# DeltaNet flow step: the gate rows move in five GpSimd transfers instead of sixteen SyncE transfers

## The chip, the core and the metric

The kernel runs on one core of a Trainium2 chip, as one program in which five engines work side by side, each through a list of its own: TensorE (PE, with its weight loads as PEld), VectorE (DVE), ScalarE (ACT), GpSimd (POOL) and SyncE (SP). SP does nothing but issue transfers. ACT and POOL issue transfers too, between their other instructions. SP's and ACT's transfers run on hardware queues, POOL's on a software queue. Every engine works strictly in the order of its list: an instruction that waits holds up everything behind it on that engine. The metric is the device time of one execution in microseconds (us).

## What is computed

One layer of a flow-matching backbone, for 128 context tokens and 512 latent tokens. A conditioning vector gives shift, scale and gate for each half of the layer; the gate multiplies the normalised output before it is added back:

```python
sh1, sc1, g1, sh2, sc2, g2 = _adaln(c, w_ada[l], b_ada[l])   # silu(c) @ w_ada + b_ada, six rows of 1024
h = _rms(xs, norm_pre1[l]) * (1 + sc1) + sh1
y = _mixer_latent(h, ...)          # neighbourhood attention + bidirectional gated DeltaNet
xs = xs + g1 * _rms(y, norm_post1[l])
xs = _ffn_sub(xs, sh2, sc2, g2, norm_pre2[l], norm_post2[l], w_ff1[l], w_ff2[l])   # uses g2 * norm_post2
```

There are two conditioning vectors (context and latent), so the kernel needs four rows of 1024 numbers: g1 and g2, each for both vectors, each multiplied by the weight of the norm behind it (norm_post1, norm_post2).

## The kernel before

All 640 tokens stay on the chip as `hhi`/`hlo` (a rounded part and the rest, so that each product is three matmuls, lines 1002 to 1004). After the first projections come three stages that matter here. The **DeltaNet stage** runs ten chunk steps (`step`, lines 787 to 874); between the small matmuls of a step, slots are filled with matmuls of a dense stream (`Unit.run`, line 994), which makes the projections of the attention and of the sigmoid gates. The **attention stage** follows, with the rest of the dense stream in its slots, and then the output projection and the MLP. In the DeltaNet stage the order on PE, DVE, ACT and SP is that in which the code is written (a manual schedule); GpSimd's order, and that of instructions that the code writes further down but that may start early, is set by a scheduler.

A unit of the dense stream loads its weights with SP into a buffer `raw` (line 172), ACT rounds them to `whi` (line 941), DVE takes the difference to `wlo` (line 945), and the buffer is free again. In the last two chunk steps two `raw` buffers are in use, so the next load waits for the difference of the unit before. A finished product lies in one of two PSUM banks `ps_mm`; ACT copies it to `gth` (line 958, three buffers), SP stores it (`gt_d`, line 972). A bank can be written again when ACT has copied it.

The **gate rows**: eight extra units give g1 and g2 as columns; DVE adds the bias and writes them into `gcol` (line 1036). `gate_rows` (line 1045), which runs in the first free bank after the last of them, loads the matching bias-free factors norm_post into a `gth` buffer called `gbn`, 32 rows of 128 numbers (line 1049), transposes `gcol` on PE into the spare columns of the bank (line 1050), multiplies the two on DVE (line 1057), and stores the 32 rows to the DRAM tensor `g_d` (line 1054). `gate_bcast` reads `g_d` back much later, in the projection and at the end. The loads and stores are cut in eight because the columns of `gcol` are kept in the order (gate and quarter, half, vector), and `g_d` in the order (gate, vector, channel).

Around it in the DeltaNet stage: line 784 loads the right-hand side of a step, line 820 loads the other direction's output of the step (`ot`, or `kt` in the last step) from `o_d`, which DVE adds at line 841 and 864; line 883 (ACT) squares the sum, line 881 loads `z_d` for the norm behind it, line 924 stores the finished output to `od_d`. The attention's first loads are issued early: `vw` (line 1246, on POOL, sixteen before the attention starts), `qk` (line 1250), `cvt` and `vctx` (line 1303) and `bias` (line 1278). `rotate` (lines 1258 to 1272) turns `qk` on DVE. Line 612 is PE's transpose of a finished output, line 1322 the first matmul of the attention's scores.

A transfer also waits for a semaphore lane: SP's and ACT's transfers share eight lanes in turn, POOL's have eight of their own. A transfer is not issued before the one eight places ahead of it in its set has landed.

Of the kernel before, what the change touches and what calls it, by code (L numbers as in the profile page):

```python
# [9 lines left out]
F32 = mybir.dt.float32  # L10
# [4 lines left out]
ALU = mybir.AluOpType  # L15
# [3 lines left out]
P = 128  # L19
# [78 lines left out]
def body(ctx: ExitStack, tc: tile.TileContext, I, O, dbg=None):  # L98
    nc = tc.nc
    dbg = dbg or {}  # L100
    V, S, G, PE = nc.vector, nc.scalar, nc.gpsimd, nc.tensor
# [31 lines left out]
    def C(n):  # L133
        i, o, w = _CW[n]
        return cst[i][:, o : o + w]

    ident = C("ident")
# [37 lines left out]
    def split(raw, kt, n, pool=None, eng=V):  # L175

        pool = pool or wpool
        hi = pool.tile([P, 1024], F32R, tag="whi", name="whi")
        lo = pool.tile([P, 1024], F32R, tag="wlo", name="wlo")
        S.copy(hi, raw)  # L180
        eng.tensor_tensor(lo, raw, hi.bitcast(F32), op=ALU.subtract)  # L181
        return [x.rearrange("p (k n) -> p k n", k=kt) for x in (hi, lo)]
# [27 lines left out]
    g_d = tc.dram_tile([2, 2, D], F32, name="g_d")  # L210
# [33 lines left out]
    def ada_mod(pc, kk, dst, bcol, nsel, pool):  # L244
        V.tensor_scalar(dst[:, 0, kk], pc[:, 0:2], b_ada[:, bcol + kk : bcol + kk + 1], None, op0=ALU.add)
        t = pool.tile([P, 2], F32, tag="adat", name="adat", bufs=2)
        V.tensor_scalar(t, pc[:, 2:4], b_ada[:, bcol + 8 + kk : bcol + 9 + kk], 1.0, op0=ALU.add, op1=ALU.add)
        V.tensor_scalar(dst[:, 1, kk], t, npre[:, nsel * 8 + kk : nsel * 8 + kk + 1], None, op0=ALU.mult)
# [53 lines left out]
    with tc.tile_pool(name="xp", bufs=1, side="right") as xp:  # L302
# [7 lines left out]
        with tc.manual_schedule(engines={mybir.EngineType.SP}):  # L310
# [29 lines left out]
            for kk in range(KT + AHEAD):  # L340
# [17 lines left out]
                for t in range(5):  # L358
                    a, w = TILES[t]
# [37 lines left out]
    for half in range(2):  # L397
        a, w = HALVES[half]
# [9 lines left out]
    for t in range(5):  # L408
        a, w = TILES[t]
# [90 lines left out]
    for x in range(3):  # L500
        sT = (kqS[:, 1], kqS[:, 0], vT)[x]
        pss = ps_tb() if x == 0 else None
        for hp in range(HP):
# [5 lines left out]
            b = cvb[mt % 2]  # L509
# [69 lines left out]
    dn = dctx.enter_context(tc.tile_pool(name="dn", bufs=1, reuse_waits="tile"))  # L579
# [200 lines left out]
    def rhs(si, m):  # L780

        r = dn.tile([P, 512], F32, tag="r", name="r", bufs=2)
        for d, (sl, mm) in enumerate(halves(si, m)):
            nc.sync.dma_start(r[sl], vs_d[d, mm, sl])
        return r
# [144 lines left out]
    class Unit:  # L930
# [63 lines left out]
        def run(self):  # L994
            if self.ch == "d":
                yield from self.branch()
            for g in () if self.ch in "dn" else range(5 if self.ch == "v" else 2):
# [13 lines left out]
                for (ch, i, c), raws in zip(self.extra, self.raws):  # L1011
                    if g == 0:
                        self.rows = dn.tile([P, 256], F32, tag="arow", name="arow", bufs=1)
                    hs = slice(128 * g, 128 * g + 128)
                    for k in range(KT):
                        q = slice(32 * (k % 4), 32 * (k % 4) + 32)
                        PE.matmul(bank[q, 320:448], csl[:, k, :], raws[k // 4][:, k % 4, hs], start=(k < 4), stop=(k >= 4),  # L1017
                                  tile_position=(0, 32 * (k % 4)))
                    reads.append(lambda: S.copy(self.rows[:, hs], bank[:, 320:448]))  # L1019
                    if g == 1:  # L1020
                        finals.append(lambda bank, ch=ch, i=i: self.columns(bank[:, 448:452], ch, i))
                        if (ch, i) == ("a", 7):
                            finals.append(gate_rows)
# [5 lines left out]
        def columns(self, pc, ch, i):  # L1029

            for j in range(2):
                PE.matmul(pc[:, 2 * j : 2 * j + 2], self.rows[:, j * 128 : j * 128 + 128], C("sel"), start=True, stop=True)
            if ch == "m":
                return lambda: ada_mod(pc, i, mod2, 24, 1, gp)
            b = b_ada[:, 16 + 24 * (i // 4) + 2 * (i % 4) :][:, 0:2].unsqueeze(2).to_broadcast([P, 2, 2])
            return lambda: V.tensor_tensor(gcol[:, i], pc.rearrange("p (i r) -> p i r", i=2), b, op=ALU.add)

        def load_extra(self):
            self.raws = [[load_raw(I["w_ada"][c, :, b * 1024 : b * 1024 + 1024], tag=t).rearrange("p (k n) -> p k n", k=4)
                          for b, t in enumerate(("whi", "wlo"))] for _, _, c in self.extra]  # L1040

    gcol = dn.tile([P, 8, 2, 2], F32, tag="gcol", name="gcol")
    finals = []

    def gate_rows(bank):

        gn = gp.tile([P, 128], F32, tag="gth", name="gbn", bufs=3)[0:32]
        for i in range(8):
            nc.sync.dma_start(gn[4 * i : 4 * i + 4], I["gate_c"][i // 4, i % 4, 1].rearrange("r (i p) -> i r p", i=2))
        PE.transpose(bank[0:32, 320:448], gcol.rearrange("p a i r -> p (a i r)"), ident)  # L1050

        def store():
            for i in range(8):
                nc.sync.dma_start(g_d[i // 4, :, i % 4 * 256 : i % 4 * 256 + 256].rearrange("r (i p) -> i r p", i=2), gn[4 * i : 4 * i + 4])

        def read():
            V.tensor_tensor(gn, gn, bank[0:32, 320:448], op=ALU.mult)
            later(0, "end", store)

        return read  # L1060
# [26 lines left out]
    def later(slots, phase, f):  # L1087
        plan.setdefault((now[0] + slots, phase), []).append(f)
# [41 lines left out]
    with tc.manual_schedule(engines={E_.PE, E_.DVE, E_.Activation, E_.SP}):  # L1130
# [35 lines left out]
        r = rhs(0, PAIRS[0])  # L1166
        for n in range(5):
# [11 lines left out]
            r = rhs(2 * n + 1, PAIRS[n])  # L1179
# [6 lines left out]
            if n < 4:  # L1186
                slot(P1, elim=3)
                r = rhs(2 * n + 2, PAIRS[n + 1])
# [47 lines left out]
    with (  # L1236
# [161 lines left out]
        with tc.manual_schedule(engines={E_.PE, E_.DVE, E_.Activation, E_.SP}):  # L1398
            late[0] = 1
            rot, oraw, subs = rotations(1, xq), [], []  # L1400
            for j in range(-2, n + 1):
                hp, b = BLK[min(j + 2, n - 1)]
# [27 lines left out]
                if j in (1, 3):  # L1430
                    for x in oraw:
                        i = len(turned_o)
# [47 lines left out]
    for c in range(4):  # L1480
# [3 lines left out]
        for mi in range(2):  # L1484
            j = 2 * c + mi
            g = gs[KT + j]
            for t0, t1 in TG:
                sl = slice(t0 * 128, t1 * 128)
                w = (t1 - t0) * 128
# [260 lines left out]
    def w2_raw(g, kh, nh):  # L1750
        return load_raw(w2(g, kh, nh))
# [159 lines left out]
    with tc.tile_pool(name="fin", bufs=2, side="right", reuse_waits="tile") as fin_:  # L1911
        gB2 = gate_bcast(1, fin_)
        w = {(kh, nh): split(w2_raw(7, kh, nh), 2, 512) for nh in range(2) for kh in range(2)}
        for blk in (None, (0, 0), (1, 0), (0, 1), (1, 1)):
            r = 0 if blk is None else 1
# [130 lines left out]
```

## Time and profile before

| | us |
|---|---|
| median of three runs | 1113.4 |
| the three runs | 1113.16, 1113.4, 1120.03 |
| profiled execution | 1112.54 |
| its span, first to last instruction | 1109.9 |
| TensorE busy in the span | 1052.8 |
| VectorE / ScalarE / GpSimd busy | 847.0 / 520.0 / 316.8 |
| mean granted TensorE clock | 0.992 of full |

The busy times are sums over the whole span; the places where PE stands still are found in the chain of waits and in the timelines. All stretches below are given in us from the start of the profiled span. "Clock" is the granted TensorE clock as a share of 2.4 GHz.

### The profile page before, as it was taken

How to read it: one execution, taken by the hardware profiler on the slowest of the kernel's cores; microseconds unless marked ns; L12 is line 12 of the kernel's file. 1: busy time of each engine (PE TensorE's matmuls, PEld its weight loads, DVE VectorE, ACT ScalarE, POOL GpSimd, SP SyncE). 2: the span in 40 equal slices, each digit the busy share in tenths (PEclk: the TensorE clock that was granted, in tenths of full speed). 3: DMA queues.
4: the chain of work that ended last, by engine and by line, in shares of the span. 5: the costliest groups of instructions: out<-in, count | busy, mean ns of one | idle time of the engine just before them, and what ended most of it. 6: DMA issues, size and time to landing. Idle time of an engine off the chain costs nothing.

```text
span 1109.9 us, 25388 instructions
## 1 busy us (share of the span) xinstructions
PE 1052.8 (95%) x10289; PEld 941.1 (85%) x10289; DVE 847.0 (76%) x1649; ACT 520.0 (47%) x1148; POOL 316.8 (29%) x275
## 2 busy tenths in 40 slices
PE   4999999989998999979999999999999999999996
PEld 3779899978987898878888999998888889797975
DVE  6567898497786686467867576899798888979785
ACT  5435443435452643327774443665444444544532
POOL 1352312000000001102514325335344353525213
PEclk9999999999999999999999999999999999999999
DMA  9832013565654655647537542465556556545605
GB/s 323 309 122 63 26 39 121 180 217 180 199 188 149 220 168 158 164 141 221 162 117 241 194 174 93 117 171 152 148 154 169 160 150 162 158 136 152 190 20 152
DMA packets 72628, 176.43 MB, mean 159 GB/s; under 512 B 18920, under 2 KB 28424, under 8 KB 72512
## 3 DMA queue, kind: packets, MB, share of 16 engines
q1 hardware_dynamic: 56320, 135.44, 36.4%
q0 software_dynamic: 9648, 24.77, 11.0%
q10 hardware_dynamic: 6544, 14.61, 4.1%
q8 instruction: 81, 1.33, 0.5%
q14 instruction: 35, 0.29, 0.1%
HBM read 150.62 MB, written 24.12 MB: 157 GB/s over the span
## 4 chain that ended last, share of the span: by engine, by line
PE 67%; DVE 21%; ACT 4%; issue 3%; DMA 3%; SPq 1%; ACTq 0%; POOL 0%; DVEq 0%; POOLq 0%
PE ps_mm L1002 5%; PE ps_mm L1004 4%; PE ps_mm L1003 4%; DVE wlo L181 4%; PE ps_mm L1646 3%; DVE y L516 3%; PE ps_mm L1644 2%; PE ps_mm L1645 2%; PE ps_mm L200 2%; DVE R L1757 2%; PE ps_mm L201 2%; PE ps_mm L202 2%; PE ps_st L1646 2%; PE ps_st L1644 2%; PE ps_st L1645 2%
## 5 line engine op out<-in xcount | busy, mean ns | idle before, releaser
L1002 PE MATMUL ps_mm<-hhi,whi 128*128 128x320 f32 x384 | 130.7, 340 | 4.9 <-ACT gth L958 4.5
L1004 PE MATMUL ps_mm<-hhi,wlo 128*128 128x320 f32 x384 | 121.3, 316 | 0.0
L1003 PE MATMUL ps_mm<-hlo,whi 128*128 128x320 f32 x384 | 121.2, 316 | 0.0
L180 ACT CAST whi<-raw 128x1024 fp32r<-128x1024 f32 x82 | 85.1, 1046 | 32.3 <-PE ps_mm L1645 8.5
L181 DVE TENSOR_TENSOR wlo<-raw,whi 128x1024 fp32r<-128x1024 f32 x59 | 81.1, 1381 | 22.0 <-ACT whi L180 21.7
L1002 PEld LDWEIGHTS ps_mm<-hhi,whi 128*128 128x128 f32 x384 | 74.6, 194 | 12.4 <-ACT gth L958 4.7
L181 POOL TENSOR_TENSOR wlo<-raw,whi 128x1024 fp32r<-128x1024 f32 x23 | 56.4, 2454 | 80.2 <-ACT whi L180 80.1
L1003 PEld LDWEIGHTS ps_mm<-hlo,whi 128*128 128x128 f32 x384 | 74.6, 194 | 0.2
L1004 PEld LDWEIGHTS ps_mm<-hhi,wlo 128*128 128x128 f32 x384 | 74.6, 194 | 0.0
L200 PE MATMUL ps_mm<-hhi,whi 128*128 128x320 f32 x192 | 60.5, 315 | 0.7 <-ACT cvb L512 0.6
L201 PE MATMUL ps_mm<-hlo,whi 128*128 128x320 f32 x192 | 59.7, 311 | 0.0
L202 PE MATMUL ps_mm<-hhi,wlo 128*128 128x320 f32 x192 | 59.4, 309 | 0.0
L181 DVE TENSOR_TENSOR wlo<-S,whi 128x1024 fp32r<-128x1024 f32 x28 | 54.9, 1979 | 4.3 <-ACT whi L180 4.2
L1246 POOL DMA_DIRECT2D vw<-v_d x32 | 21.1, 676 | 128.8 <-ACT arow L1019 94.6
L181 DVE TENSOR_TENSOR wlo<-T,whi 128x1024 fp32r<-128x1024 f32 x28 | 43.9, 1567 | 15.2 <-ACT whi L180 15.2
L654 POOL DMA_DIRECT2D rls<-ai_d x10 | 5.4, 540 | 174.5 <-PE ps_tb L617 160.2
L945 DVE TENSOR_TENSOR wlo<-raw,whi 128x1024 fp32r<-128x1024 f32 x35 | 42.7, 1221 | 10.9 <-ACT whi L941 10.4
L516 DVE SCALAR_TENSOR_TENSOR y<-cvb,cw,y 128x644 f32<-128x644 f32 x48 | 45.4, 945 | 0.9
L180 ACT CAST whi<-T 128x1024 fp32r<-128x1024 f32 x28 | 29.4, 1049 | 33.9 <-PE ps_mm L1645 16.2
L180 ACT CAST whi<-S 128x1024 fp32r<-128x1024 f32 x28 | 28.8, 1051 | 23.9 <-PE ps_tb L202 12.3
L941 ACT CAST whi<-raw 128x1024 fp32r<-128x1024 f32 x35 | 36.5, 1047 | 7.1 <-issue 6.1
L958 ACT ACTIVATE gth<-ps_mm 128x320 f32<-128x320 f32 x32 | 13.9, 436 | 55.4 <-PE ps_mm L1017 38.2
(577 smaller groups left out, 3533.5 us busy)
## 6 DMA issues: line engine op xcount, KB each, us to landing
raw<-in_w_ff_dram SPq DMA_DIRECT2D x57, 512.0 KB
raw<-in_w_ada_dram SPq DMA_DIRECT2D x48, 512.0 KB
raw<-in_w_gate_dram SPq DMA_DIRECT2D x16, 512.0 KB
S<-in_w_ff_dram SPq DMA_DIRECT2D x14, 512.0 KB
T<-in_w_ff_dram SPq DMA_DIRECT2D x14, 512.0 KB
S<-in_w_ff_dram POOLq DMA_DIRECT2D x14, 512.0 KB, 5.6
T<-in_w_ff_dram POOLq DMA_DIRECT2D x14, 512.0 KB, 7.2
raw<-in_w_dn_dram SPq DMA_DIRECT2D x12, 512.0 KB
```

Source lines behind the costliest of these rows:

```text
L180: S.copy(hi, raw)
L181: eng.tensor_tensor(lo, raw, hi.bitcast(F32), op=ALU.subtract)
L200: PE.matmul(out, ah, bh, start=(i == 0), stop=False)
L201: PE.matmul(out, ah, bl, start=False, stop=False)
L202: PE.matmul(out, al, bh, start=False, stop=(i == n - 1))
L516: V.scalar_tensor_tensor(y, b[:, j : j + 644], cw[:, mt * 5 + j : mt * 5 + j + 1], y, op0=ALU.mult, op1=ALU.add)
L1002: PE.matmul(ps, ah, bh, start=(k == 0), stop=False)
L1003: PE.matmul(ps, ah, bl, start=False, stop=False)
L1004: PE.matmul(ps, al, bh, start=False, stop=(k == KT - 1))
L1644: PE.matmul(o, hi[:, k, fs], bh, start=(first and k == 0), stop=False, skip_group_check=not first)
L1645: PE.matmul(o, hi[:, k, fs], bl, start=False, stop=False, skip_group_check=not first)
L1646: PE.matmul(o, lo[:, k, fs], bh, start=False, stop=(k == 3), skip_group_check=not first)
```

## The change

The columns of `gcol` are kept in the order in which the rows of `g_d` follow each other: gate, vector, quarter, half. With that, the 32 rows of `gbn` are one contiguous block of `g_d`, so that one transfer stores them all, and four transfers of eight rows load the factors. All five are issued by GpSimd in place of SyncE.

```diff
-            return lambda: V.tensor_tensor(gcol[:, i], pc.rearrange("p (i r) -> p i r", i=2), b, op=ALU.add)
+            return lambda: V.tensor_tensor(gcol[:, i // 4, :, i % 4].rearrange("p r i -> p i r"), pc.rearrange("p (i r) -> p i r", i=2), b, op=ALU.add)
...
-    gcol = dn.tile([P, 8, 2, 2], F32, tag="gcol", name="gcol")
+    gcol = dn.tile([P, 2, 2, 4, 2], F32, tag="gcol", name="gcol")
...
-        for i in range(8):
-            nc.sync.dma_start(gn[4 * i : 4 * i + 4], I["gate_c"][i // 4, i % 4, 1].rearrange("r (i p) -> i r p", i=2))
-        PE.transpose(bank[0:32, 320:448], gcol.rearrange("p a i r -> p (a i r)"), ident)
+        for i in range(4):
+            nc.gpsimd.dma_start(gn[8 * i : 8 * i + 8], I["gate_c"][i // 2, :, 1, i % 2].rearrange("j (i p) -> j i p", i=2))
+        PE.transpose(bank[0:32, 320:448], gcol.rearrange("p w r j i -> p (w r j i)"), ident)

         def store():
-            for i in range(8):
-                nc.sync.dma_start(g_d[i // 4, :, i % 4 * 256 : i % 4 * 256 + 256].rearrange("r (i p) -> i r p", i=2), gn[4 * i : 4 * i + 4])
+            nc.gpsimd.dma_start(g_d.rearrange("w r (i p) -> (w r i) p", i=8), gn)
```

Lines behind line 1054 move up by one. The lists of PE and ACT hold the same instructions in the same order as before. Three lists differ.

SP, in the ninth and tenth chunk step, from the right-hand side of the last step (line 784) to the load of the other direction's output into `kt` (line 820), before:

```order
L784 DMA r<-vs_d 64x512 x2
L1049 DMA gbn<-in_gate_c_dram 4x1x128 x8
L172 DMA raw<-in_w_gate_dram 128x1024
L924 DMA od_d<-oT 128x4x64 x2
L972 DMA gt_d<-gth 128x320
L1054 DMA g_d<-gbn 2x2x128 x8
L820 DMA kt<-o_d 64x512 x2
L972 DMA gt_d<-gth 128x320
```

and after:

```order
L784 DMA r<-vs_d 64x512 x2
L172 DMA raw<-in_w_gate_dram 128x1024
L924 DMA od_d<-oT 128x4x64 x2
L972 DMA gt_d<-gth 128x320
L820 DMA kt<-o_d 64x512 x2
L972 DMA gt_d<-gth 128x320
```

The sixteen small transfers ahead of the weights and ahead of the `kt` load are gone; nothing else between them moved.

POOL, the same stretch: its list here is transfers only, the sixteen `vw` loads and then the attention's, before:

```order
L1246 DMA vw<-v_d 128x1x128 x16
L1278 DMA bias_7155<-in_bias_dram 128x256
L1278 DMA bias_7156<-in_bias_dram 128x256
L1250 DMA qk_7428<-qk_d 128x640
L1423 DMA oraw<-od_d 128x640 x2
```

and after:

```order
L1245 DMA vw<-v_d 128x1x128 x15
L1049 DMA gbn<-in_gate_c_dram 8x1x128 x4
L1245 DMA vw<-v_d 128x1x128
L1053 DMA g_d<-gbn 32x128
L1277 DMA bias_7144<-in_bias_dram 128x256
L1277 DMA bias_7145<-in_bias_dram 128x256
L1422 DMA oraw<-od_d 128x640 x2
L1249 DMA qk_7417<-qk_d 128x640
```

The gate rows' loads stand ahead of the last `vw` load and their store behind it; one `qk` load (for the third head pair) went behind the two `oraw` loads.

DVE, from the first `rotate` (line 1258 before, 1257 after) to the sum of the last step's output (line 864), before:

```order
L1258 STREAM_SHUFFLE xs<-qk_7149 128x512
L1263 TENSOR_TENSOR xs<-xs,rope 128x512
L1265 TENSOR_TENSOR qk_7149<-qk_7149,rope 128x512
L1268 TENSOR_TENSOR qb<-qk_7149,xs 128x8x4x16
L841 TENSOR_TENSOR kt<-kt,qS 128x512
L892 TENSOR_REDUCE fs_6897<-kt 128x8
L1258 STREAM_SHUFFLE xs<-qk_7151 128x512
L1289 MEMSET bias_7157 128x128
L1289 MEMSET bias_7158 128x128
L893 TENSOR_TENSOR fs_6897<-fs_6897,rq_114 128x8
L945 TENSOR_TENSOR wlo<-raw,whi 128x1024
L864 TENSOR_TENSOR kt<-kt,ps_st_6928 128x512
```

and after:

```order
L1257 STREAM_SHUFFLE xs<-qk_7138 128x512
L841 TENSOR_TENSOR kt<-kt,qS 128x512
L892 TENSOR_REDUCE fs_6886<-kt 128x8
L1262 TENSOR_TENSOR xs<-xs,rope 128x512
L1264 TENSOR_TENSOR qk_7138<-qk_7138,rope 128x512
L893 TENSOR_TENSOR fs_6886<-fs_6886,rq_114 128x8
L1267 TENSOR_TENSOR qb<-qk_7138,xs 128x8x4x16
L1257 STREAM_SHUFFLE xs<-qk_7140 128x512
L945 TENSOR_TENSOR wlo<-raw,whi 128x1024
L864 TENSOR_TENSOR kt<-kt,ps_st_6917 128x512
L1288 MEMSET bias_7146 128x128
L1288 MEMSET bias_7147 128x128
```

Three instructions of the rotation, which stood ahead of line 841, now stand between line 841 and line 864; two memsets went behind line 864.

## Rows read from the trace of the kernel before

**Rows 1.** The chain that ended last, 440 to 520: start, length, what.

```profile
457.91 10.54 DMA bias<-in_bias_dram
...
471.09 1.81 DMA gbn<-in_gate_c_dram
473.29 1.21 DVE wlo L945
...
482.15 5.02 DMA kt<-o_d
487.27 0.69 DVE kt L841
...
491.83 0.43 ACT gth L958
```

**Rows 2.** Timeline of SP's queue: start, length, line, transfer, count.

```profile
463.25 8.45 SPq L1049 DMA_DIRECT2D gbn<-in_gate_c_dram  x8
474.52 0.35 SPq L172 DMA_DIRECT2D raw<-in_w_gate_dram  x1
...
476.64 4.92 SPq L1054 DMA_DIRECT2D g_d<-gbn  x8
481.60 1.14 SPq L820 DMA_DIRECT2D kt<-o_d  x2
```

**Rows 3.** Timeline of PE; in brackets the idle time before, and its releaser.

```profile
473.41 0.41 PE L1002 MATMUL ps_mm<-hhi,whi 128*128 128x320 f32 x1 [0.39 <-DVE gbn L1057]
...
475.98 1.15 PE L828 MATMUL ps_st<-r,YZ 64*64 64x64 f32 x32 [0.99 <-issue]
...
492.31 0.64 PE L1002 MATMUL ps_mm<-hhi,whi 128*128 128x320 f32 x1 [4.47 <-ACT gth L958]
...
498.80 0.66 PE L612 MATMUL ps_tb<-cst,kt 128*128 128x128 f32 x4
```

**Rows 4.** Windows, PE: window, length, busy (instructions), granted clock, DMA share, GB/s.

```profile
492.30:495.60 3.30, 3.29 (x12) 0.50 0.86 304
```

**Rows 5.** Timeline of DVE around the gate rows.

```profile
473.08 0.28 DVE L1057 TENSOR_TENSOR gbn<-gbn,ps_mm 32x128 f32<-32x128 f32 x1 [5.11 <-DMA gbn<-in_gate_c_dram]
...
479.89 0.69 DVE L1268 TENSOR_TENSOR qb<-qk,xs 128x512 f32<-128x512 f32 x1
487.27 0.69 DVE L841 TENSOR_TENSOR kt<-kt,qS 128x512 f32<-128x512 f32 x1 [6.69 <-DMA kt<-o_d]
...
497.15 0.69 DVE L913 TENSOR_TENSOR kt<-kt 128x512 f32<-128x512 f32 x1
```

**Rows 6.** Timeline of ACT and its queue.

```profile
468.65 1.04 ACT L941 CAST whi<-raw 128x1024 fp32r<-128x1024 f32 x1
...
481.50 0.33 ACTq L1250 DMA_DIRECT2D qk<-qk_d  x1
```

**Rows 7.** Timeline of POOL.

```profile
455.36 5.20 POOL L1246 DMA_DIRECT2D vw<-v_d  x8 [26.82 <-PE ps_tp L743]
499.76 1.16 POOL L1278 DMA_DIRECT2D bias<-in_bias_dram  x2 [39.20 <-DVE st L1340]
```

**Rows 8.** Line 1246 alone, 455 to 461: from issue to landing.

```profile
DMA to landing us min/median/max: 5.2/7.0/9.3
```

**Rows 9.** Line 655 alone, ten 12 KB loads on POOL's queue.

```profile
DMA to landing us min/median/max: 1.8/2.1/5.4
```

**Rows 10.** Windows, all engines: busy of PE, PEld, DVE, ACT, POOL, clock, DMA share, GB/s.

```profile
459.00:461.00 2.00, 1.32 (x32) 1.19 (x32) 1.97 (x6) 2.00 (x9) 1.56 (x3) 1.00 1.02 265
...
469.00:471.00 2.00, 2.00 (x53) 1.81 (x55) 0.00 (x0) 0.69 (x1) 0.00 (x0) 1.00 0.01 2
...
477.00:479.00 2.00, 2.00 (x18) 1.94 (x14) 1.80 (x4) 0.00 (x0) 0.00 (x0) 1.00 0.99 290
```

**Rows 11.** The same, in the attention stage.

```profile
500.00:520.00 20.00, 20.00 (x158) 17.94 (x157) 16.14 (x45) 13.45 (x34) 5.19 (x10) 1.00 0.73 220
```

**Rows 12.** The tile gcol: durations (ns, min/median/max) and starts.

```profile
L1036 DVE TENSOR_TENSOR gcol<-ps_mm,b_ada x8: 150/154/163, 350.6 to 459.9; 128x4 f32<-128x4 f32 x8
```

## The prediction, made before the changed kernel ran

> **What bounds the kernel now.** PE is busy 1052.8 of 1109.9 us, so I read first the chain that ended last, to find the places where it leaves PE; the change touches only one stretch, 455 to 500, the last two chunk steps of DeltaNet. There the chain runs for 35 us almost wholly through transfers. It begins with a bias load on ACT's queue, which takes 10.54 us and lands at 468.45 [rows 1]. The sixteen small gate transfers stand behind it: SP is occupied by the eight loads from 463.25 to 471.70 [rows 2], although each is a 2 KB transfer, because a transfer waits for the landing of the one eight places ahead of it, and the bias loads were ahead. The last gate load lands at 472.90 [rows 1]. DVE has then stood 5.11 us in front of line 1057 [rows 5], with the difference of line 945 behind it, and that difference frees the weight buffer for SP's next load, which starts at 474.52 [rows 2], just after it ends (473.29 + 1.21) [rows 1]. Behind that SP spends 4.92 us on the eight gate stores, and only at 481.60 comes to the `kt` load of line 820 [rows 2]. This lands at 487.17 [rows 1], and DVE has waited 6.69 us for it in front of line 841 [rows 5]. Line 864 follows, ACT's square (line 883) waits for that, and behind the square in ACT's list stands the copy that empties the PSUM bank PE needs. So PE stands still for 4.47 us until 492.31, and the 12 matmul slots after that run at the 1.2 GHz level (granted 0.50) for 3.3 us [rows 3, 4]. Two smaller PE waits belong to the same chain: 0.39 us for line 1057 itself, and 0.99 us at 475.98, in front of line 828, whose right-hand side DVE finished late behind line 1057 [rows 3]. PE's three waits are 5.85 us together.
>
> **Step 1, the gate loads on POOL.** GpSimd issues its second eight `vw` loads from 455.36 in 5.20 us, 0.65 each [rows 7], so the first gate load goes out at about 459.9, behind seven of them, and POOL has nothing else until 499.76 [rows 7]. The second to fourth loads wait on their lanes for the first three of these `vw`, which by the shortest and the median landing, 5.2 and 7.0 us [rows 8], arrive at 460.6 to 463.7. The fourth gate load then goes out at about 464. How long it takes is not in the trace. Bounds: the lightest row is the 2.1 us of a 12 KB load on this queue [rows 9], which gives 466; the heaviest is the 9.3 us of a `vw` [rows 8], which gives 473.3. I take 469.2, where the last `vw` landed (459.9 + 9.3): by the window 469 to 471 all transfers had drained (DMA share 0.01) [rows 10], and 16 KB more will hardly shift that. DVE needs them for line 1056, behind line 864 of the step before, but the difference behind it cannot start before ACT's rounding ends at 469.69 (468.65 + 1.04) [rows 6]. So up to 469.4 the loads are hidden; 473.3 would cost 3.9 us of what follows.
>
> **Step 2, SP without the sixteen.** The difference runs 469.7 to 470.9, SP's weight load starts at 470.9 instead of 474.52. From there to the first gate store SP needed 476.64 - 474.52 = 2.12 us [rows 2]; now the `kt` load stands there: 473.0 instead of 481.60, **8.6 us earlier** (3.6 from the loads, 4.96 from the stores).
>
> **Step 3, the `kt` load.** It took 487.17 - 481.60 = 5.57 us [rows 1, 2], against the attention's first loads from ACT's queue (481.50 [rows 6]); that gives 478.6. Now those come later (below), but weights and two stores are still in flight ahead: before, they drained about 2.6 us after the last was issued (the window 477 to 479 is still full, DMA share 0.99 [rows 10]). Bounds: 476.6 (drained, then 256 KB at that window's 290 GB/s) and 481.2 (5.57 + 2.6). I take 478.6.
>
> **Step 4, DVE's new order.** Three rotation instructions of 0.69 us [rows 5] now stand between line 841 and line 864, where before they filled the wait. That is 2.1 us, less 0.3 for two memsets moved back: 1.8 us. ACT's copy started 491.83 - 487.27 = 4.56 us after line 841 [rows 1], now about 6.4: at 485.0. PE restarted 0.48 us behind it (492.31 - 491.83), so the bank is ready at 485.5. ACT's five transfer issues ahead of the square (0.33 us for the row shown [rows 6]) now wait for the last rotation, 3.4 us behind line 841, and need about 2.4 us: done at 5.8, as line 864 ends, so at most 0.3 us more.
>
> **Step 5, PE.** Without 0.39 and 0.99, less 0.2 us of gaps that stay, PE is 1.2 us earlier and wants the bank at 487.84 - 1.2 = 486.6 (492.31 - 4.47 = 487.84). The bank is ready at 485.5 to 485.8: no wait, by 0.8 us. So the 4.47 goes, and with it the half clock behind it: 12 matmuls in 3.3 us [rows 4], which at the 2.4 GHz level take half, so 1.6 goes; I take 1.4, since the first after a change of work is longer at full clock too (0.41 at 473.41 [rows 3]). **Sum: 1.2 + 4.5 + 1.4 = 7.1 us.**
>
> **What is late next.** Behind it PE needs line 912/913's output for the transpose of line 612, at 498.80 before [rows 3], 491.7 now. DVE ended line 913 at 497.84, 10.57 us after line 841 began [rows 5]; with the three rotations (2.1) it ends 12.7 us after 478.6, at 491.3: just in time. From there PE is 20.00 of 20 us busy [rows 11], and what feeds it is itself triggered by PE or DVE, so the 7 us should last to the end.
>
> **Edits with no cost.** POOL's store waits for line 1056 (about 469.5) and behind it wait the last `vw` and bias loads: the `vw` leaves at about 465 instead of 459.9, and its reader is in the attention's second head pair, tens of us away; without that cover it would cost a landing, 9.3 us at most. The store's landing (5.4 us at most by [rows 9], so 475.5) is waited for by the ACT copy that takes over `gbn`'s buffer, at about 479. The `qk` load behind the two `oraw` loads comes two issues later, 1.2 us by [rows 7], and what `oraw` waits for its data; its reader is the third head pair's rotation, so I count it as hidden; if it isn't, that is a case of "given back" below. `gcol` still takes eight DVE writes of 0.15 us [rows 12]; were the new stride to double them, 1.2 us over 110 us of shared DVE time.
>
> **Rivals.** *Late by a part.* The gate loads land at 473.3 (3.9 us past the 469.4 of step 1), or the `kt` load at 481.2 (2.6 late). The bank is then ready 3.9 or 2.6 us later, PE waits 3.0 or 1.7 us for it, and the half clock (1.4) returns: gains of 2.7 and 4.0, about 1109.9. With both late (`kt` at 485.1) nothing is left, 1113.2. For it: the window at 459 to 461 was full (DMA share 1.02). Against: everything had drained by 469 [rows 10].
>
> *Issue held up.* DVE's instructions hold up GpSimd's issuing. If each of the four gate loads waited out one DVE instruction of 0.69 us [rows 5], they would come 2.8 us later, at 472.0, 2.6 past the point where they cost: PE waits 1.7 and loses the clock, 1109.5. Against: the eight `vw` issues kept a steady 0.65 us each while DVE was busy 1.97 of 2.00 us [rows 7, 10]. The Trainium skill ("SBUF — State Buffer", section "Summary: rules for kernel authors") speaks against this move: it says that descriptors of GpSimd's transfers are starved while DVE runs in its faster modes, and advises ACT's or SP's queue. Its section "Who interferes with whom" takes tensor_tensor out of that, and by that the trace agrees. By the page's 3.1 us in place of 0.62 for one such transfer, an estimate, the sum would lose about the same as by the rows.
>
> *Given back.* The attention's DVE work is late next and PE waits there for what it gained: 1113. For it: DVE is busy 16 of 20 us [rows 11] and the margin at line 612 is 0.4 us. Against: no PE wait shows in that window.
>
> *Slower.* In the new order line 841 stands in front of the rotation, and DVE's in-order list makes the rotation, ACT's `qk` load and all behind it wait for the `kt` load. If this landed no earlier than now, the copy would come 1.8 us later than before and PE with it: 1113.4 + 1.8 = 1115.2. It decides from 487.27 - 1.8 = 485.5: a `kt` load later than that loses time. That takes 6.9 us more than step 3; only gate loads landing after 476 do it.
>
> *More.* Earlier weights remove waits that I don't see: 1103 or less. Against: the three PE waits are all that the chain has here.
>
> **How the numbers follow.** The profiled execution took 1112.54, the median is 0.9 above it. 1112.54 - 7.1 = 1105.4; on the median, 1113.4 - 7.1 = **1106.3**. Chances: forecast (1105 to 1108) 0.60, late by a part 0.17, issue held up 0.02, given back 0.11, slower 0.04, more 0.06. The range leaves out "more" and "slower" and takes in the unknown costs up to both bounds: **1103.5 to 1113.5**. One per cent, 11 us, is about what a measurement of this kernel can tell from no change; the forecast and all rivals but the far end of "more" lie within it, and the slower one is worth only 2 us. Faster by more 0.04, within 0.93, slower by more 0.03, the last for what I don't see.
>
> **What would show it.** In the profile after: no 4.47 us PE wait for `gth`, and full clock from 486 to 492 (step 5); the DVE wait at the gate multiply under 2 us (step 1); the `kt` load issued at about 473 and landed by 479 (steps 2, 3); line 864 about 5 us behind line 841 (step 4); line 612's transpose at about 491.7 instead of 498.80, and the same 7 us at the span's end. The prediction is wrong if the `kt` load lands after 480, if PE stops for a bank again, or if the 7 us is there at 500 and gone at the end.

## The result, and the profile after

| | before | after |
|---|---|---|
| median, 20 runs each (us) | 1116.62 | 1107.49 |
| lowest and highest | 1113.14, 1120.39 | 1102.86, 1114.22 |
| profiled execution, its span | 1112.54, 1109.9 | 1107.69, 1105.9 |

The ratio is 0.992, with a 95% interval of 0.9906 to 0.9935: 7.3 to 10.5 us less. Forecast were 7.1 us less and 1106.3 us. The rows of after stand below; its axis runs 5.6 us behind that of before at 458 and 4.05 us behind it at 467, since the stretches ahead of the change took another time in the two executions (the last section shows one cause), so distances are read, not times.

SP's queue after, to be held against [rows 2]:

```profile
477.22 0.34 SPq L172 DMA_DIRECT2D raw<-in_w_gate_dram  x1
477.60 0.98 SPq L924 DMA_DIRECT2D od_d<-oT  x2
478.63 0.65 SPq L972 DMA_DIRECT2D gt_d<-gth  x1
479.32 1.13 SPq L820 DMA_DIRECT2D kt<-o_d  x2
```

From the weight load to the `kt` load SP now needs 479.32 - 477.22 = 2.10 us, before 481.60 - 474.52 = 7.08. The 4.92 us of stores are gone and nothing has taken their place.

POOL after, to be held against [rows 7], and behind it, from the view of line 1049 alone, the landing of its four loads:

```profile
460.95 4.55 POOL L1245 DMA_DIRECT2D vw<-v_d  x7 [26.28 <-PE ps_tp L743]
465.50 0.56 POOL L1049 DMA_DIRECT2D gbn<-in_gate_c_dram  x1
467.19 0.56 POOL L1049 DMA_DIRECT2D gbn<-in_gate_c_dram  x1 [1.14 <-DMA vw<-v_d]
469.19 0.55 POOL L1049 DMA_DIRECT2D gbn<-in_gate_c_dram  x1 [1.44 <-DMA vw<-v_d]
469.90 0.55 POOL L1049 DMA_DIRECT2D gbn<-in_gate_c_dram  x1 [0.16 <-issue]
476.34 0.53 POOL L1053 DMA_DIRECT2D g_d<-gbn  x1 [4.73 <-DVE gbn L1056]
```

```profile
DMA to landing us min/median/max: 5.8/6.7/8.9
```

The loads wait on their lanes for `vw` transfers to land, as step 1 had it, and need 5.8 to 8.9 us each. DVE after, against [rows 5]:

```profile
471.34 0.68 DVE L864 TENSOR_TENSOR kt<-ot,ps_st 128x512 f32<-128x512 f32 x1
475.78 0.27 DVE L1056 TENSOR_TENSOR gbn<-gbn,ps_mm 32x128 f32<-32x128 f32 x1 [3.76 <-DMA gbn<-in_gate_c_dram]
484.60 0.69 DVE L841 TENSOR_TENSOR kt<-kt,qS 128x512 f32<-128x512 f32 x1 [2.56 <-DMA kt<-o_d]
489.62 0.68 DVE L864 TENSOR_TENSOR kt<-kt,ps_st 128x512 f32<-128x512 f32 x1
```

ACT after, the rounding ahead of the difference, the copy that releases PE's 0.91 us wait below, and the copy that empties the bank, against [rows 6] and the copy of [rows 1]:

```profile
472.70 1.04 ACT L941 CAST whi<-raw 128x1024 fp32r<-128x1024 f32 x1
...
477.43 0.50 ACT L958 ACTIVATE gth<-ps_mm 128x320 f32<-128x320 f32 x1
...
490.92 0.91 ACT L958 ACTIVATE gth<-ps_mm 128x320 f32<-128x320 f32 x2
```

PE after, against [rows 3]: the only two waits of its list between 470 and 500.

```profile
477.98 0.42 PE L1002 MATMUL ps_mm<-hhi,whi 128*128 128x320 f32 x1 [0.91 <-ACT gth L958]
497.21 0.65 PE L612 MATMUL ps_tb<-cst,kt 128*128 128x128 f32 x4 [0.75 <-DVE kt L913]
```

PE's 4.47 us wait for the bank is gone; 0.91 and 0.75 us stand in its stretch. The half clock of [rows 4] is gone too. Windows of PE after (window, length, busy, clock, DMA share, GB/s):

```profile
472.00:484.00 12.00, 11.09 (x170) 1.00 0.63 173
484.00:496.00 12.00, 11.96 (x96) 1.00 0.57 176
```

And the chain that ended last, after, against [rows 1]:

```profile
461.60 7.30 DMA vw<-v_d
...
469.90 5.80 DMA gbn<-in_gate_c_dram
...
479.85 4.66 DMA kt<-o_d
```

It still goes through the gate loads, now behind a `vw` transfer instead of the bias.

### The profile page after: what moved, and what is told of

Read it like the earlier page. It is cut to its first block, busy times and chain, and to the rows that moved or that the text cites. A ratio compares the mean times of both kernels' runs of the same rounds, so it can differ in the third digit from the quotient of the medians.

```text
span 1105.9 us, 25384 instructions
## 1 busy us (share of the span) xinstructions
PE 1054.2 (95%) x10289; PEld 942.8 (85%) x10289; DVE 846.3 (77%) x1649; ACT 520.6 (47%) x1148; POOL 317.0 (29%) x280
## 4 chain that ended last, share of the span: by engine, by line
PE 69%; DVE 21%; DMA 3%; ACT 3%; issue 3%; SPq 0%; POOL 0%; DVEq 0%; ACTq 0%; POOLq 0%
PE ps_mm L1002 5%; PE ps_mm L1004 4%; PE ps_mm L1003 4%; DVE wlo L181 4%; PE ps_mm L1645 3%; PE ps_mm L1644 3%; PE ps_mm L1643 3%; PE ps_mm L201 2%; PE ps_mm L200 2%; PE ps_mm L202 2%; DVE y L516 2%; DVE R L1756 2%; PE ps_st L1644 2%; PE ps_st L1645 2%; PE ps_st L1643 2%
## 5 line engine op out<-in xcount | busy, mean ns | idle before, releaser
L180 ACT CAST whi<-T 128x1024 fp32r<-128x1024 f32 x28 | 29.4, 1049 | 34.2 <-PE ps_mm L1644 16.5
L516 DVE SCALAR_TENSOR_TENSOR y<-cvb,cw,y 128x644 f32<-128x644 f32 x48 | 42.6, 887 | 0.9
```

The source lines that it names most:

```text
L516: V.scalar_tensor_tensor(y, b[:, j : j + 644], cw[:, mt * 5 + j : mt * 5 + j + 1], y, op0=ALU.mult, op1=ALU.add)
```

## The experiments

**Theory:** the kernel is shortened by as much as the `kt` load of line 820 starts earlier, because PE's bank hangs on it; who issues the gate transfers, and how many they are, counts only by what stands ahead of that load. **Rivals:** the queue or the number of transfers is what counts; the loads alone (or the stores alone) bring it; or the change also speeds up the MLP, since GpSimd's later transfers stand on other lanes.

One stretch, the same in every kernel, measures the place of the change without the scatter of the rest: from the start of line 864 on DVE in the ninth step (471.34 above) to the start of DVE's third reciprocal of the attention (line 1348 before, 1347 after). In the first profile of before it is

```profile
467.29 0.68 DVE L864 TENSOR_TENSOR kt<-ot,ps_st 128x512 f32<-128x512 f32 x1
513.57 0.16 DVE L1348 RECIPROCAL st<-st 128x2 f32<-128x2 f32 x1
```

and in that of after it ends with

```profile
512.00 0.16 DVE L1347 RECIPROCAL st<-st 128x2 f32<-128x2 f32 x1
```

so 513.57 - 467.29 = 46.28 us before and 512.00 - 471.34 = 40.66 after. All eleven runs and the two first profiles, ordered by when SP starts the `kt` load after that line 864 (before: 481.60 - 467.29 = 14.31; after: 479.32 - 471.34 = 7.98):

| kernel | kt load after | stretch | PE waits for the bank | ratio to before (interval) |
|---|---|---|---|---|
| before with five idle GpSimd loads (e_pool5) | 14.83 | 47.79 | 5.11 | 1.000 (0.9975 to 1.0024) |
| before | 14.31 | 46.28 | 4.47 | |
| before, again (x_before) | 13.99 | 47.26 | 4.53 | 1.000 (0.9985 to 1.0015) |
| loads on GpSimd, stores on SP (e_loads_only) | 11.98 | 44.09 | 2.06 | 0.993 (0.9905 to 0.9955) |
| stores behind the kt load (e_defer) | 9.91 | 42.86 | 0.58 | 0.9939 (0.9913 to 0.9965) |
| store on GpSimd, loads on SP (e_stores_only) | 9.18 | 41.96 | 0.53 | 0.9947 (0.9926 to 0.9967) |
| after, store in four (e_eight) | 8.12 | 41.16 | 0.58 | 0.9932 (0.9907 to 0.9956) |
| after | 7.98 | 40.66 | 0 | 0.992 (0.9906 to 0.9935) |
| after, third time (x_after2) | 7.84 | 39.64 | 0 | 0.9911 (0.9881 to 0.9942) |
| the five on SP (e_five_sp) | 7.61 | 40.29 | 0 | 0.9923 (0.9894 to 0.9951) |
| after, again (x_after) | 6.59 | 39.51 | 0 | 0.9915 (0.9892 to 0.9937) |
| loads early, all on SP (e_early_sp) | 6.48 | 38.99 | 0 | 0.9922 (0.9898 to 0.9945) |
| loads early, on GpSimd (e_early) | 5.80 | 38.85 | 0 | 0.9914 (0.9885 to 0.9943) |

But for two pairs of neighbours the stretch follows the start of the `kt` load, whichever edit moved it. One thing besides that start differs between the kernels, DVE's order: line 864 follows line 841 by 3.25 us in before, 3.8 in e_loads_only, 4.3 in e_stores_only, e_defer, e_five_sp and the two early versions, and 5.0 in after and e_eight. From the mean of the three of before (14.38 and 47.11) to that of the three of after (7.47 and 39.94) it is 6.9 us of start for 7.2 us of stretch.

**The changed kernel again (x_after).** No edit.

> The changed kernel once more, for a second profile and a second ratio on another chip. Theory (the sixteen SyncE transfers held back the kt load; with them gone PE's 4.47 us wait for the bank and the half clock behind it go): ratio 0.992 to 0.995 (5.6 to 8.9 us), no PE wait over 1 us for gth near 490, and the instructions from 510 to 600 about 5.6 us ahead of where the place 455 of the same run would put them in the first pair of profiles. Rival 'more elsewhere' (the change also takes about 2.5 us out of the MLP, because GpSimd's transfers are counted through their lanes differently): the offset against before grows by the same 2 to 3 us again between 740 and the end. If that is only a difference between two executions, the offset there changes by some other amount, of either sign.

The ratio, 0.9915, is a little better than expected; PE has no wait for `gth` near 490. The stretch is 39.51 us, 6.8 us under the first of before. Between 563 and the end, DVE's same instructions move ahead of those of before by 1.65 us more, in the first profile of after by 2.47: this kept the rival alive.

**The store alone (e_stores_only).**

```diff
-        for i in range(4):
-            nc.gpsimd.dma_start(gn[8 * i : 8 * i + 8], I["gate_c"][i // 2, :, 1, i % 2].rearrange("j (i p) -> j i p", i=2))
+        for i in range(8):
+            nc.sync.dma_start(gn[4 * i : 4 * i + 4], I["gate_c"][i // 4, 2 * (i % 2) : 2 * (i % 2) + 2, 1, i // 2 % 2].rearrange("j (i p) -> j i p", i=2))
```

> Half of the change: the store is one transfer on GpSimd, the loads are eight transfers on SyncE as before. Theory: SyncE's loads hold its weight load as before (it starts near 474.5 on the axis of before), but the 4.92 us of stores ahead of the kt load are gone, so kt starts near 476.7 and lands near 482; the bank is ready about 5 us less the 1.8 us of the new order earlier, PE's wait is 1 us or less, its small waits of 0.39 and 0.99 stay. Gain 4 to 5.5 us, ratio 0.995 to 0.9965. Rival 'the loads are what counts': 1.5 us or less, ratio 0.9985 or more. Rival 'more elsewhere' (the number of GpSimd transfers): a gain that in the MLP is not that of the changed kernel.

SP in that kernel, and PE's wait for the bank behind it:

```profile
467.58 8.44 SPq L1049 DMA_DIRECT2D gbn<-in_gate_c_dram  x8
...
480.97 1.16 SPq L820 DMA_DIRECT2D kt<-o_d  x2
```

```profile
492.71 0.41 PE L1002 MATMUL ps_mm<-hhi,whi 128*128 128x320 f32 x1 [0.53 <-ACT gth L958]
```

This is as expected: the eight loads hold SP 8.44 us as in [rows 2], the `kt` load still comes 5.1 us sooner after line 864 (9.18 for 14.31), and the bank wait is 0.53. The stretch is 5.2 us under the mean of before, and the ratio 0.9947, a little better than the 0.995 to 0.9965 expected, is 3.7 to 8.3 us.

**The loads alone (e_loads_only).**

```diff
-            nc.gpsimd.dma_start(g_d.rearrange("w r (i p) -> (w r i) p", i=8), gn)
+            for i in range(8):
+                nc.sync.dma_start(g_d.rearrange("w r (i p) -> (w r i) p", i=8)[4 * i : 4 * i + 4], gn[4 * i : 4 * i + 4])
```

> The other half: the four loads on GpSimd, the store as eight transfers on SyncE. Theory: the weight load is released as in the changed kernel, some 2 to 3 us earlier than before, but the kt load still stands behind about 4.9 us of stores: it starts 2 to 3.6 us earlier than before, PE's wait falls from 4.47 to 1 to 2.5 us and the half clock may stay. Gain 2 to 4 us, ratio 0.9965 to 0.998. Rival 'the loads are what counts': the whole gain, 0.992 to 0.994. Rival 'the stores alone count': nothing, 0.999 to 1.001.

PE there, ACT's copies at that time, and PE's windows:

```profile
490.71 0.70 PE L1322 MATMUL ps_tp<-qk,qb 64*128 64x256 f32 x4 [2.06 <-DVE qk L1272]
```

```profile
490.69 0.75 ACT L958 ACTIVATE gth<-ps_mm 128x320 f32<-128x320 f32 x2
```

```profile
491.90:493.90 2.00, 2.00 (x11) 0.62 0.99 360
493.90:495.90 2.00, 2.00 (x10) 0.53 0.29 78
```

The wait is 2.06 us, inside the 1 to 2.5 expected, and the half clock stays. It is put down to line 1322, because the scheduler set the attention's scores eight matmul groups earlier in this kernel; the bank's copy begins only at 490.69, so PE would have waited for it as well. The stretch is 3.0 us under the mean of before. The ratio, 0.993, is better than the 0.9965 to 0.998 expected. It lies where the rival "the loads are what counts" put it (0.992 to 0.994), and its interval, 5.0 to 10.6 us, does not reach down to the stretch's 3.0. So the timing does not tell this half from the whole; only the profile, with its bank wait and half clock, speaks against that rival, and the difference stays open (below). Together the two halves give 5.2 + 3.0 = 8.2 us, for 7.2 of both; 1 us is within the scatter of the three stretches of before (46.28 to 47.79).

**All five on SP (e_five_sp).** Both `nc.gpsimd.dma_start` of the change become `nc.sync.dma_start`.

> The same five transfers in the new order of columns, all issued by SyncE. Theory: what counts is how many transfers stand ahead of the weight load and the kt load, not whose queue has them: eleven fewer take about 2 us out of the loads and 4.3 us out of the stores, the kt load starts 6 us or more earlier than before and PE does not wait for the bank. Gain 5 to 8 us, ratio 0.993 to 0.9955, like the changed kernel. Rival 'the queue counts': half of the gain or less, ratio 0.9965 or more.

```profile
465.49 5.37 SPq L1049 DMA_DIRECT2D gbn<-in_gate_c_dram  x4
...
476.37 0.34 SPq L1053 DMA_DIRECT2D g_d<-gbn  x1
476.75 1.14 SPq L820 DMA_DIRECT2D kt<-o_d  x2
```

These are SP's rows of that kernel. It is the same as after, in stretch (40.29 against a mean of 39.94) and in ratio, a little better than expected. The queue is not what counts; since DVE's order differs here (above), the closer test of that is the pair of early versions below.

**Before, again (x_before).** No edit.

> The kernel before once more, for a second profile of it: how much of the difference between two profiles of before and after is only the difference of two executions. Theory (the change's own gain, at its place, is 5 to 6 us; half clock near 461 to 465 comes and goes): ratio 0.998 to 1.002; PE again waits 4.2 to 4.7 us for gth near 490 on the axis of the first, with half clock behind it; the MLP's PE waits for wlo (4.1 us in the first profile of before, 2.0 and 2.7 in the two of after) lie anywhere from 2 to 4.5. Rival 'more elsewhere' (the change also speeds up the MLP, by the number of GpSimd transfers before it): they are 4.1 us again, within 0.4.

The ratio is 1.000. The bank wait is 4.53 us and the stretch 0.98 us longer than in the first profile. PE's windows behind the wait show why, first in the first profile of before, then in this one:

```profile
492.30:496.30 4.00, 4.00 (x17) 0.58 0.72 252
```

```profile
496.04:500.04 4.00, 4.00 (x15) 0.50 0.69 254
500.04:504.04 4.00, 4.00 (x24) 0.74 0.02 4
```

The half clock behind the wait took 4 x 0.42 = 1.7 us of PE's work there, and 2.0 + 1.0 = 3.0 here. PE waits 3.8 us for `wlo` in the MLP, as both theories allow.

**The store in four (e_eight).**

```diff
-            nc.gpsimd.dma_start(g_d.rearrange("w r (i p) -> (w r i) p", i=8), gn)
+            for i in range(4):
+                nc.gpsimd.dma_start(g_d.rearrange("w r (i p) -> (w r i) p", i=8)[8 * i : 8 * i + 8], gn[8 * i : 8 * i + 8])
```

> The changed kernel with its store cut in four: eight transfers on GpSimd in place of five, so that every later GpSimd transfer stands on the lane it has in the kernel before. Theory: three more small stores on a queue that nobody waits for at that time; the gain at its place is that of the changed kernel, ratio 0.990 to 0.994. Rival 'more elsewhere' (the lanes of the later GpSimd transfers): the MLP's PE waits for wlo are back at 3.9 to 4.5 us, and 1.5 to 2.5 us of the gain are gone, ratio 0.993 to 0.996.

The ratio lies where both theories put it. The MLP's waits for `wlo` are 2.9 us, under the 3.9 that the lanes demand; from 563 to the end it gained 1.34 us. The lanes are not it. PE's 0.58 us at the bank are there because line 841 comes 0.54 us later behind the first line 864 than in after (13.80 for 13.26): the `kt` load starts 0.14 us later and takes 5.68 us to it for 5.28. Whether the three more stores lengthen the load is not shown.

**The loads early (e_early).** `gn` becomes the memory of a tile that is dead by then, and the four loads are issued where `gcol` is made.

```diff
+    gn = ba.rearrange("p t c -> p (t c)")[0:32, 0:128]
+    for i in range(4):
+        nc.gpsimd.dma_start(gn[8 * i : 8 * i + 8], I["gate_c"][i // 2, :, 1, i % 2].rearrange("j (i p) -> j i p", i=2))
...
-        gn = gp.tile([P, 128], F32, tag="gth", name="gbn", bufs=3)[0:32]
-        for i in range(4):
-            nc.gpsimd.dma_start(gn[8 * i : 8 * i + 8], I["gate_c"][i // 2, :, 1, i % 2].rearrange("j (i p) -> j i p", i=2))
```

> The changed kernel, with the four loads issued hundreds of us earlier into memory that is free by then, so that nothing waits for them; the store is the same one on GpSimd. Theory: in the changed kernel the gate loads still land about 2 us after ACT's rounding, so DVE's 2.4 to 3.8 us wait in front of the gate multiply shrinks to what ACT's rounding leaves (about 1 to 2 us), SyncE's weight load and kt load come 1.5 to 2.5 us earlier still, and PE's 0.91 and 0.75 us waits go or shrink: 0.5 to 1.5 us better than the changed kernel, ratio 0.989 to 0.993. Rival 'the loads' landing cost nothing': equal to the changed kernel at its place, within 0.3 us.

DVE in that kernel, and the one wait of PE in the stretch:

```profile
471.00 0.28 DVE L1056 TENSOR_TENSOR ba<-ba,ps_mm 32x128 f32<-32x128 f32 x1 [0.81 <-ACT gth L958]
471.94 1.23 DVE L945 TENSOR_TENSOR wlo<-raw,whi 128x1024 fp32r<-128x1024 f32 x1 [0.66 <-ACT whi L941]
479.43 0.69 DVE L841 TENSOR_TENSOR kt<-kt,qS 128x512 f32<-128x512 f32 x1 [0.57 <-DMA kt<-o_d]
```

```profile
476.99 1.15 PE L828 MATMUL ps_st<-r,YZ 64*64 64x64 f32 x32 [0.42 <-issue]
```

Now ACT's rounding releases the difference, as step 1 wanted it, the `kt` load is 0.57 us late instead of 2.56, and PE's waits in the stretch are 0.42 us for 0.91 and 0.75. Its stretch is 1.1 us under the mean of after, the shortest of all; line 864 also follows line 841 by 0.7 us less here. The timing (0.9914) cannot tell it from after.

**The stores behind the kt load (e_defer).** Before, with one number changed, so that the eight stores run four matmul slots later: `later(0, "end", store)` becomes `later(4, "end", store)`.

> The kernel before with all its sixteen transfers on SyncE and the old columns, but the eight stores issued four slots later, behind the kt load. Theory (it is the place of the stores ahead of the kt load that costs, not their number or queue): as with the store on GpSimd alone, the kt load starts about 4.9 us earlier than before, PE's wait for the bank is 1 us or less, gain 3.5 to 5 us, ratio 0.9955 to 0.997. Rival 'the number of transfers counts': nothing gained, 0.999 to 1.001, or a loss if what stands behind the stores now (the next gt_d store, a weight load) is late.

SP in that kernel, and PE and ACT behind it:

```profile
482.62 1.15 SPq L820 DMA_DIRECT2D kt<-o_d  x2
...
494.04 6.43 SPq L1054 DMA_DIRECT2D g_d<-gbn  x8
```

```profile
494.41 0.42 PE L1002 MATMUL ps_mm<-hhi,whi 128*128 128x320 f32 x1 [0.58 <-ACT gth L958]
```

```profile
501.84 0.44 ACT L958 ACTIVATE gth<-ps_mm 128x320 f32<-128x320 f32 x1 [3.65 <-DMA g_d<-gbn]
```

All sixteen transfers, the old columns and SP as their issuer are kept (the scheduler changed DVE's order with it, which by itself puts line 864 1.1 us later behind line 841), and the stretch is 4.25 us shorter than the mean of before, with a bank wait of 0.58; the ratio, 0.9939, is better than expected. So it is the place of the stores that cost, not their number. They now occupy SP for 6.43 us where nobody on the chain waits; an ACT copy into `gbn`'s buffer waits 3.65 us for them, without PE standing still for it.

**Before with five idle GpSimd loads (e_pool5).** It issues five loads of gate rows into memory that nobody reads again, early in the program; the lists of PE, DVE and SP are those of before.

```diff
+        for i in range(5):
+            nc.gpsimd.dma_start(spare[8 * i : 8 * i + 8], I["gate_c"][i % 4 // 2, :, 1, i % 2].rearrange("j (i p) -> j i p", i=2))
```

> The kernel before with all its sixteen transfers, and five transfers of the same size more on GpSimd, early in the program, into memory that nobody reads again: the number of GpSimd transfers ahead of the MLP is that of the changed kernel, and nothing else of the change is made. Theory (what is gained outside of the place of the change is the scatter of single executions): ratio 0.9985 to 1.0015, PE's waits for wlo in the MLP 3.8 to 4.4 us as in the profiles without added GpSimd transfers, the stretch from 540 to the end within 0.4 us of before. Rival 'more elsewhere' (the number of GpSimd transfers sets how well the MLP's sums run): those waits are 2 to 3 us and the stretch from 540 to the end is 0.6 to 2.5 us shorter.

The ratio is 1.000, PE's waits for `wlo` are 3.5 us, and 0.48 us are gained from 563 to the end: this is between the two theories, and near to the first. The number of GpSimd transfers alone brings nothing that the timing shows. The half clock behind the bank wait took 4 x 0.50 = 2.0 us here:

```profile
494.72:498.72 4.00, 4.00 (x15) 0.50 0.71 258
```

**Early loads, all on SP (e_early_sp).** This is e_early with `nc.sync` in both places. The lists of PE, DVE and ACT are those of e_early.

> The kernel with the loads issued early, but the four loads and the store on SyncE; the lists of PE, DVE and ACT are the same as with GpSimd, so this is the queue alone. Theory (it is what stands ahead of the kt load that counts): one store of about 0.4 us ahead of the kt load, gain at the place within 0.5 us of the kernel with early loads on GpSimd (7.4 us against the first profile of before, from 467 to 538), PE without a wait for the bank, ratio 0.989 to 0.994. Rival 'the queue counts': 2 us or more less. Rival 'more elsewhere': the stretch from 540 to the end as in before within 0.4 us, since GpSimd has no transfer more.

The stretch is 38.99 against 38.85, without a bank wait. From 563 to the end it gained 0.50 us with no GpSimd transfer added, e_early with its five 0.64. For the stretch, the queue is worth 0.14 us.

**The changed kernel a third time (x_after2).** No edit.

> The changed kernel a third time, for the scatter of its profiles. Theory: ratio 0.990 to 0.994; at the place (467 to 538) 5 to 7 us less than the first profile of before; PE's waits for wlo in the MLP and the stretch from 540 to the end anywhere between those of before and the two profiles of after. Rival 'more elsewhere': the stretch from 540 to the end is again 1.6 to 2.5 us shorter than in before, and PE waits 2 to 2.7 us for wlo there.

PE's waits for `wlo` from 540 to the end (us, times, longest) in after, and then in x_after2:

```profile
PE ps_mm L1645 <- DVE wlo L181: 2.0, 4, 0.8
```

```profile
PE ps_mm L1645 <- DVE wlo L181: 3.6, 5, 1.3
```

The same program gives 2.0 and 3.6 us (x_after 2.7), and gains of 2.47, 1.65 and 1.01 us from 563 to the end; before, x_before and e_pool5 wait 4.1, 3.8 and 3.5 us and differ by 0.48 us there. Over all thirteen profiles the five kernels without an added GpSimd transfer wait 3.8 to 4.4 us (before 4.1, x_before 3.8, e_defer 3.9, e_five_sp 4.4, e_early_sp 3.8), the eight with one or more 2.0 to 3.7 (e_loads_only 3.7, e_stores_only 3.4, e_early 3.2, e_eight 2.9 and those above). From 563 to the end the five gain -0.3 to 0.5 us, the eight 0.5 to 2.5. So about 1 us in the MLP that goes with the GpSimd transfers is likely; but e_pool5, which adds nothing else, gains only 0.48 us, e_five_sp is timed like after without any, and how it would come about is not shown.

## Why the prediction was right, and where a step was off

**The sum** was 7.1 us, and at the place of the change it is 7.2 (means of three profiles each). That it fits to the tenth is luck, since the terms moved against each other, and so is the median: the forecast of 1106.3 us started from 1113.4, the median of three runs, where twenty give 1116.62, and 7.1 us lies just under the interval of the timed gain (7.3 to 10.5). The mechanism, a bank that hangs on the `kt` load, is what the experiments bear out.

| term | predicted | three of before, less three of after |
|---|---|---|
| small waits of PE | 1.2 | 1.42 - 1.16 = 0.3 |
| wait for the bank | 4.5 | 4.70 |
| half clock behind it | 1.4 | (1.7 + 3.0 + 2.0) / 3 = 2.2 |

The small waits of before are 1.38, 0.99 and 1.90 us, those of after 1.66, 0.91 and 0.91. The 0.91 is a wait that the sum did not have. The unit of line 1002, which in the first profile of before waited for the gate multiply (0.39 us), waits in after for ACT's copy of the unit just ahead of it, 477.43 + 0.50 = 477.93. The gate multiply had ended at 475.78 + 0.27 = 476.05. It is the same 0.91 us in all three profiles, whether DVE waits 2.38 or 3.76 us for the gate loads; in x_after the multiply ended 2.4 us before PE stood still:

```profile
476.97 0.28 DVE L1056 TENSOR_TENSOR gbn<-gbn,ps_mm 32x128 f32<-32x128 f32 x1 [2.38 <-DMA gbn<-in_gate_c_dram]
```

```profile
480.55 0.42 PE L1002 MATMUL ps_mm<-hhi,whi 128*128 128x320 f32 x1 [0.91 <-ACT gth L958]
```

The kernels that have this wait for the copy are those in which GpSimd loads the gate rows at that place (after, e_loads_only, e_eight); e_five_sp, whose DVE waits 2.88 us for the same loads from SP, has none. Why this unit waits for ACT's copy in them is not shown.

**Step 1** is the one that failed. The issue of the fourth load was right (469.90 less 5.6 is 464.3, forecast 464), its landing was not: it came 1.96 us after ACT's rounding had ended (475.70 against 472.70 + 1.04), where the prediction had it 0.5 us ahead. DVE's wait shrank from 5.11 to 3.76 us (2.4 and 3.6 in the other two), not to under 2. That is the rival "late by a part" by half. What it cost is a later difference, and with it a later weight load and `kt` load (step 2); the room left in step 5 took it up. That the loads' landing is what holds the difference is shown by e_early, where DVE's wait for them goes and the `kt` load starts 5.80 us after line 864.

**Step 2:** the stores' part holds to the tenth (2.10 us from weight load to `kt` load, forecast 2.12); the loads' part, 3.6 us, was 0.9 to 2.3 us too large. The `kt` load starts 8.0, 6.6 and 7.8 us after line 864, where the step had 473.0 - 467.29 = 5.71. **Step 3** was a little long: 484.60 - 479.32 = 5.28 us from issue to line 841 for 5.57, 4.40 in x_after2, and in x_after (4.02) DVE found the data there. By a sign of its own the prediction is wrong in the first profile: the `kt` load landed at 479.85 + 4.66 = 484.51, on the axis of before 480.46, which is after 480 (in the other two it was there by 479.6). PE did not stop for a bank even so. **Step 4:** line 864 follows line 841 by 5.02 us (about 5 forecast) and the copy by 6.32 (6.4).

**Step 5** came out, but with less room than its 0.8 us: the copy starts 490.92 - 471.34 = 19.6 us after line 864, the bank is ready 0.5 us later, and PE, itself held up by the 0.91, comes just then. e_eight, 0.54 us later with its line 841, waits 0.58. **What is late next** was line 612, as forecast: 0.75 us in the first profile, nothing in the other two.

**Rivals.** *Issue held up:* no. POOL spends 0.55 to 0.56 us on each gate load, less than on a `vw`, and each gap ahead of one but the last ends with a `vw` landing. The Trainium skill ("SBUF — State Buffer", section "Summary: rules for kernel authors") would have GpSimd's descriptors starved by DVE's faster modes; no run here shows that. *Given back:* no, the offset from 510 to 600 is constant at -1.57 us. *Slower:* no; it needed a `kt` load landing within 1.8 us of the old time, and that started 6.3 to 7.7 us sooner after line 864. *More:* no, the median is 1107.49.

**Open:** the timed gain is larger than the stretch. The three ratios of the changed kernel (0.992, 0.9915, 0.9911) are 8.9 to 9.9 us, the stretch 7.2, which would be 0.9936: inside two of the three intervals, at the edge of the third. In the other seven kernels that gain, the timed gain is larger too, by 0.6 to 4.8 us, most in e_loads_only (7.8 against 3.0).

The profiles' own spans differ by less, on average 5.8 us: 1109.9, 1114.6 and 1112.3 of the three of before, 1105.9, 1108.2 and 1105.2 of the three of after. These 5.8 are 7.2 in the stretch and 1.4 from 563 on, less 2.8 that after loses ahead of the first line 864. That line came at 467.29, 471.28 and 468.53 in before and at 471.34, 473.91 and 470.24 in after; all thirteen profiles lie between 467.29 and 473.91 without an order by edit, so the 2.8 us are taken for scatter, and without them the profiles would give 8.6 us. The timed runs agree: the profiled executions of before were 4.1, 0.1 and 2.4 us faster than the medians of their runs, at a mean granted clock of 0.989 where the 67 timed ones that list it have 0.986; those of after were 0.2, 1.1 and 0.4 us slower, at 0.988 where 32 timed ones have 0.990. A longer half clock behind the bank wait in before's timed runs, as in x_before, would fit too. Which of these it is was not shown, nor why e_loads_only gains most beyond its stretch.

## What to carry to other kernels

A transfer costs what it holds up in its queue, so ask first what stands behind it: here one number that lets eight stores run behind the `kt` load shortens the stretch by 4.25 us with all sixteen kept. Moving small loads to another queue moves them behind that queue's own transfers; issued early into dead memory they wait for nobody. Cutting a stretch out of the profile between two instructions that every version has tells versions apart that the whole time cannot.

## What was not expected of the hardware

The half clock comes and goes in the same program. Two windows of PE in x_after, and the same two in x_after2, which runs 2.1 us ahead of it at 458:

```profile
461.00:465.00 4.00, 3.97 (x88) 1.00 0.80 214
466.50:470.50 4.00, 3.93 (x40) 0.57 1.06 275
```

```profile
461.00:465.00 4.00, 2.65 (x32) 1.00 1.05 293
466.50:470.50 4.00, 4.00 (x83) 1.00 1.11 246
```

x_after falls to half clock behind PE's 1.28 us wait in front of line 828, x_after2 does not, with the same wait of 1.28 us. Such a drop is worth about 1.5 us: from line 828 to line 864 it is 473.91 - 466.25 = 7.66 us in x_after, and 470.24 - 464.11 = 6.13 in x_after2. Between the first profiles of before and after one such difference, between 461 and 467, lies ahead of anything that the change does.

And the shape of a store counts for its issue. Eight stores of four rows that lie together (e_loads_only, first) occupy SP's queue for 239 to 331 ns each; the eight of before, the same bytes in the old order of columns, for 565 to 626 (ns, min/median/max, first and last start):

```profile
L1054 SPq DMA_DIRECT2D g_d<-gbn x8: 239/242/331, 477.0 to 480.3; - x8
```

```profile
L1054 SPq DMA_DIRECT2D g_d<-gbn x8: 565/566/626, 476.6 to 481.0; - x8
```
